# Softmax values of a layer in one pass of 512 columns, first scores 128 wide, differences of h ordered behind its last split

## The chip, the cores and the metric

The kernel runs on one core of one Trainium2 chip. The metric is the device time of one launch in microseconds (us); for the kernel before, three runs gave a median of 1129.27 us (1129.11 to 1130.02). Engines are named as the profile names them: PE is TensorE's matmul, PEld its load of the stationary operand, DVE is VectorE, ACT is ScalarE, POOL is GpSimd, SP is SyncE, which issues most DMAs.

## What is computed

Two layers over 512 tokens of 1024 columns, all in float32. Each layer normalizes x, makes one joint projection, runs two kinds of attention on it (eight stick-breaking heads and four differential heads with a softmax), projects back, and adds a squared-ReLU MLP. Cut to what matters here:

```python
for l in range(DEPTH):                      # DEPTH = 2
    h = rmsnorm(x, attn_norm[l])
    proj = jnp.einsum('bsd,de->bse', h, w_in[l])        # 1024 -> 3072
    sb_q, sb_k, sb_v, df_q, df_k, df_v = jnp.split(proj, splits, axis=-1)
    ...
    s = jnp.einsum('bhmqd,bhmkd->bhmqk', qblk, kh) * scale      # query blocks of 128
    p = jax.nn.softmax(jnp.where(allowed, s, neg), axis=-1)
    attn = p[:, :, 0] - lam * p[:, :, 1]
    df_heads = jnp.einsum('bhqk,bhkd->bhqd', attn, vh)          # vh: the softmax values, df_v
    ...
    x = x + jnp.einsum('bse,ed->bsd', mixed, w_o[l])
    h = rmsnorm(x, mlp_norm[l])
    u = jnp.square(jax.nn.relu(jnp.einsum('bsd,df->bsf', h, w_ff1[l])))
    x = x + jnp.einsum('bsf,fd->bsd', u, w_ff2[l])
return rmsnorm(x, final_norm)
```

Both attentions are causal: query block i (128 tokens) needs the keys of blocks 0 to i alone.

## The kernel before

**Precision.** Every product of two float32 operands is made of three matmuls in a rounded float32 type (float32r): each operand is split into a high part (ACT, a copy into float32r, L115, L237, L248) and the rest (DVE, a subtraction, L131, L238, L249). `three` (L297 to L299) issues high·high, high·low and low·high into one PSUM bank. The scores alone use two (L528, L529).

**Weights.** `_Weights` streams the weights through as units of 512 KB (128 x 1024): SP loads a unit into one of three `raw` buffers (L108), ACT and DVE split it into `whi` and `wlo` (two pairs of buffers; the first two units behind a layer's start go to the buffers `mdh`, `mdl`, which are free until the heads' outputs need them), and PE uses it. `_unit_list` fixes the order of the units, and `ORDER` the order of the projection's blocks in a layer: "d" is the q and k of one softmax head with its two maps, "s" of two stick-breaking heads (two units, 24 matmuls of 512 columns for each), "w" and "u" the values of half of the heads of each kind (two units).

**The projection's order.** Before the change a layer goes d0, w0, d1, d2, d3, w2, s0, u0, s1, s2, s3, u2. `values_of` makes the values of one half of the heads: 256 columns for each of four token blocks, two token blocks to a bank, and for each chunk c of the 1024 inputs three matmuls with 128 tokens of h as the stationary operand and 256 columns of weights as the moving one (L437 to L439). `evict_v` (L419 on ACT, L420 on DVE) scales them by the norm's factor `rcol` and splits them into `vdh`, `vdl` (softmax) or `vs` (stick-breaking).

**Attention between the projection.** `attn` is a generator of 24 units of attention (per layer 8 of softmax heads, 16 of stick-breaking ones), which the loop over `dense` calls in between the projection's matmuls, as far as a budget allows and once a block's q and k are ready. The stages of a unit: scores (`scores`, L528 and L529, into the three PSUM banks named "s"), softmax or sigmoids on ACT and DVE, transposes on PE two units later (L616), and the product with the values three units later (into the bank "o"). Between a block's matmuls and its scores lie the rotation (L496, L497, L504, L505 on DVE), a split, and twelve DMAs from SP (`move`, L465) which bring the halves into the stacks `st` and `kl`. PSUM has eight banks: two "t" (transposes), two "mm" (projection), three "s", one "o".

**Widths.** `scores` for query block i multiplies the keys of blocks 0 to i, 128·(i+1) columns, but never fewer than 256: block 0 multiplies 256 columns and reads 128 of them.

**The end of the attention part.** `wo(0)` projects back: for each of eight chunks db, DVE adds to x (L755), `make_h` forms the MLP's h (ACT L248, DVE L249), and `add_sq` sums the squares (L257, L258). The MLP's first matmuls (`f`) follow at once and read h chunk by chunk. The later groups of the MLP use sums and differences of halves of h, which `h_form` and `scaled` make (ACT L986, DVE L979); in layer 0 they are written over x, behind DMAs that park x in DRAM.

**What sets the order.** The program is written in the order that the generators give, and a scheduler then places each engine's instructions by their dependencies; `behind(a, b)` adds an order between two instructions without a wait on data. Each engine works through its own queue in order.

Of the kernel before, what the change touches and what calls it, by code (L numbers as in the profile page):

```python
# [30 lines left out]
ORDER = ("d0", "w0", "d1", "d2", "d3", "w2", "s0", "u0", "s1", "s2", "s3", "u2")  # L31
# [19 lines left out]
def _unit_list():  # L51
# [112 lines left out]
def trunk(ctx, tc, opened, xT, w, w2, w1, gfin, lamv, cos, sin, out):  # L164
# [129 lines left out]
    def three(pt, a, b, first, last, goes_on=False):  # L294
        ah, al = a
        bh, bl = b
        nc.tensor.matmul(pt, ah, bh, start=first, stop=False, skip_group_check=goes_on)  # L297
        nc.tensor.matmul(pt, ah, bl, start=False, stop=False, skip_group_check=goes_on)  # L298
        nc.tensor.matmul(pt, al, bh, start=False, stop=last, skip_group_check=goes_on)  # L299
# [33 lines left out]
    for l in range(L):  # L333
        with ExitStack() as actx:
# [75 lines left out]
            def evict_v(pt, kind, b, half):  # L410
                for n in range(2):
                    tb = 2 * half + n
                    src, r = pt[:, 256 * n : 256 * n + 256], rcol[:, tb : tb + 1]
                    if kind == "u":
                        hi, lo = (vs[:, tb, 2 * b : 2 * b + 4, a : a + 64] for a in (0, 64))
                        src = src.rearrange("p (h e) -> p h e", h=4)
                    else:
                        hi, lo = (v[:, tb, b * P : (b + 2) * P] for v in (vd_hi, vd_lo))
# [3 lines left out]
                if half == 1:  # L422
                    for i in (b, b + 1):
                        ready[("vs" if kind == "u" else "vd", i)] = clock[0] + 2.5

            def values_of(kind, b, tags):
                pts = [bank(tag, f"p{l}{kind}{b}{half}") for half, tag in enumerate(tags)]
                for part in range(2):
                    u = W.next("v")
                    for half, pt in enumerate(pts):  # L430
                        for n in range(4):
                            c = 4 * part + n
                            wh, wl = wpair(u, n, 256)
                            for q in range(2):
# [4 lines left out]
                                W.product = nc.tensor.matmul(  # L439
                                    o, h_lo[:, c, t], wh, start=False, stop=c == KC - 1 and q == 1)  # L440
                            if c == KC - 1:
                                evict_v(pt, kind, b, half)
                            yield

# [77 lines left out]
            def scores(pt, st, m, i):  # L522
                wd = P * (i + 1)
                wp = max(wd, 256)
# [217 lines left out]
            def wo(half):  # L742
                for j in range(4):
                    u = W.next("o")
                    for dd in range(2):
# [10 lines left out]
                        if half == 0:  # L756
                            make_h(db, gcol("mlp", l, db))
# [3 lines left out]
            def dense(pts):  # L761
# [74 lines left out]
        with ExitStack() as fctx:  # L836
# [140 lines left out]
            def scaled(out, c0, half, other, op):  # L977
                for c in range(4):
                    nc.vector.scalar_tensor_tensor(  # L979
                        out=out[:, c, :], in0=x[:, c0 + c, half], scalar=gcol("mlp", l, c0 + c), in1=other[:, c, :],  # L980
                        op0=ALU.mult, op1=op)
# [305 lines left out]
def _layout(inputs):  # L1287
# [4 lines left out]
    for i, n in enumerate(_RING):  # L1292
# [7 lines left out]
        elif kind == "v":  # L1300
            blk = w_in[l, 512 * u[3] : 512 * u[3] + 512, u[2] : u[2] + 256]
        elif kind == "o":
# [58 lines left out]
```

## Time and profile before

| | us |
|---|---|
| median of three runs | 1129.27 |
| the profiled execution | 1129.41 |
| its span, from the first to the last instruction | 1127.6 |
| PE busy | 1118.6 (99%), 6613 matmuls |
| DVE busy | 904.9 (80%) |
| ACT busy | 686.8 (61%) |
| POOL busy | 148.1 (13%) |
| mean granted clock of PE | 0.998 |

Read it with care in one point: a matmul's row lasts from its start to its modelled end, and the rows of neighbours overlap. What a matmul costs in a full queue is the distance from its start to the next one's start. In the timeline a row is: start, length, engine, line, operation, output<-inputs, shape of the stationary operand, shape of the output, how many; in brackets stands how long the engine was idle before, and what released it.

### The profile page before, as it was taken

The numbers are of one execution on the slowest core, as the hardware profiler recorded it, in microseconds if no ns is written. First come the engines' busy times: TensorE is split into PE (matmuls) and PEld (weight loads), VectorE is DVE, ScalarE is ACT, GpSimd is POOL, SyncE is SP. The second block draws the span as 40 slices with busy tenths as digits, with TensorE's granted clock in tenths as the row PEclk, the third lists the DMA queues.
The fourth block names the chain that finished last, engine by engine and source line by source line (L and its number), as shares of the span: only waits on it lengthen the run. The fifth ranks groups of instructions, "written<-read, shape, count | busy, mean of one in ns | idle before, by whom it ended". The sixth has DMA issues, their size and how long they took to land.

```text
span 1127.6 us, 17680 instructions
## 1 busy us (share of the span) xinstructions
PE 1118.6 (99%) x6613; PEld 990.2 (88%) x6613; DVE 904.9 (80%) x1317; ACT 686.8 (61%) x1115; POOL 148.1 (13%) x233
## 2 busy tenths in 40 slices
PE   9999999999999999999999999999999999999997
PEld 7899889878899899899888998898888998998986
DVE  7897788788658878779878977887876787797787
ACT  6456666567558458466344666665765484674665
POOL 1001343101011001001000013330010110010010
PEclk9999999999999999999999999999999999999999
DMA  7665363259777678757326643622477886687462
GB/s 253 157 181 150 88 175 103 76 192 242 191 205 178 174 209 179 190 139 206 112 75 187 169 132 112 166 78 75 149 183 218 209 187 178 184 187 202 116 131 94
DMA packets 61045, 181.28 MB, mean 161 GB/s; under 512 B 7456, under 2 KB 8736, under 8 KB 60960
## 3 DMA queue, kind: packets, MB, share of 16 engines
q1 hardware_dynamic: 50160, 141.84, 40.3%
q0 software_dynamic: 10368, 37.75, 19.2%
q8 instruction: 52, 0.85, 0.3%
q10 hardware_dynamic: 432, 0.56, 0.1%
q14 instruction: 33, 0.27, 0.1%
HBM read 150.77 MB, written 4.19 MB: 137 GB/s over the span
## 4 chain that ended last, share of the span: by engine, by line
PE 97%; DVE 1%; issue 1%; DMA 0%; ACT 0%; POOL 0%; SPq 0%; POOLq 0%; DVEq 0%
PE X L297 9%; PE X L298 9%; PE X L299 9%; PE V L297 4%; PE V L298 4%; PE V L299 4%; PE wo L297 3%; PE wo L299 3%; PE wo L298 3%; PE f L298 2%; PE f L299 2%; PE f L297 2%; PE Y L297 2%; PE Y L299 2%; PE Y L298 2%; PE W L299 1%
## 5 line engine op out<-in xcount | busy, mean ns | idle before, releaser
L115 ACT ACTIVATE whi<-q 128x1024 fp32r<-128x1024 f32 x96 | 101.6, 1059 | 109.8 <-PE X L299 37.9
L131 DVE TENSOR_TENSOR wlo<-q,whi 128x1024 fp32r<-128x1024 f32 x96 | 117.0, 1222 | 49.4 <-ACT whi L115 49.4
L115 ACT ACTIVATE whi<-raw 128x1024 fp32r<-128x1024 f32 (+1 forms) x82 | 80.9, 992 | 46.6 <-issue 20.3
L131 DVE TENSOR_TENSOR wlo<-raw,whi 128x1024 fp32r<-128x1024 f32 (+1 forms) x82 | 95.4, 1169 | 10.4 <-ACT whi L115 10.0
L297 PE MATMUL X<-whi,Ah 128*128 128x512 f32 x248 | 97.6, 394 | 0.0
L298 PE MATMUL X<-wlo,Ah 128*128 128x512 f32 x248 | 96.6, 390 | 0.0
L299 PE MATMUL X<-whi,Al 128*128 128x512 f32 x248 | 96.6, 389 | 0.0
L131 DVE TENSOR_TENSOR wlo<-waves,whi 128x1024 fp32r<-128x1024 f32 x40 | 48.9, 1222 | 17.0 <-ACT whi L115 16.8
L115 ACT ACTIVATE whi<-waves 128x1024 fp32r<-128x1024 f32 x40 | 42.2, 1055 | 31.0 <-PE X L299 18.2
L297 PEld LDWEIGHTS X<-whi,Ah 128*128 128x128 f32 x248 | 46.6, 188 | 11.9 <-DVE y L1091 1.9
L299 PEld LDWEIGHTS X<-whi,Al 128*128 128x128 f32 x248 | 46.6, 188 | 9.8
L298 PEld LDWEIGHTS X<-wlo,Ah 128*128 128x128 f32 x248 | 46.6, 188 | 8.8
L299 PE MATMUL X<-h_hi,wlo 128*128 128x256 f32 x192 | 54.3, 283 | 0.0
L297 PE MATMUL X<-hxh,whi 128*128 128x256 f32 x192 | 54.3, 283 | 0.0
L298 PE MATMUL X<-hxl,whi 128*128 128x256 f32 x192 | 54.3, 283 | 0.0
L299 PE MATMUL X<-hxh,wlo 128*128 128x256 f32 x192 | 54.3, 283 | 0.0
L298 PE MATMUL X<-h_lo,whi 128*128 128x256 f32 x192 | 54.3, 283 | 0.0
L297 PE MATMUL X<-h_hi,whi 128*128 128x256 f32 x192 | 54.3, 283 | 0.0
L298 PE MATMUL f<-h_lo,whi 128*128 128x512 f32 x128 | 49.9, 390 | 0.5 <-DVE h_lo L249 0.5
L297 PE MATMUL f<-h_hi,whi 128*128 128x512 f32 x128 | 50.4, 394 | 0.0
L299 PE MATMUL f<-h_hi,wlo 128*128 128x512 f32 x128 | 49.9, 390 | 0.0
L238 DVE TENSOR_TENSOR Al<-x,Ah 128x512 fp32r<-128x512 f32 (+1 forms) x60 | 46.6, 793 | 3.8 <-ACT Ah L237 3.5
(748 smaller groups left out, 3794.9 us busy)
## 6 DMA issues: line engine op xcount, KB each, us to landing
raw<-in_w SPq DMA_DIRECT2D x78, 512.0 KB, 3.8
q<-in_w SPq DMA_DIRECT2D x48, 512.0 KB, 4.8
q<-in_w POOLq DMA_DIRECT2D x48, 512.0 KB, 7.8
waves<-in_w SPq DMA_DIRECT2D x28, 512.0 KB, 4.9
first_a<-in_w SPq DMA_DIRECT2D x12, 512.0 KB, 4.4
first_b<-in_w SPq DMA_DIRECT2D x12, 512.0 KB, 5.2
first_c<-in_w SPq DMA_DIRECT2D x12, 512.0 KB, 4.3
first_b<-in_w POOLq DMA_DIRECT2D x12, 512.0 KB, 7.1
```

Source lines behind the costliest of these rows:

```text
L115: return self.nc.scalar.activation(o, src, AF.Copy)
L131: self.last = h, nc.vector.tensor_tensor(out=lo[:, a:b], in0=raw[:, a:b], in1=hi[:, a:b].bitcast(F32), op=ALU.subtract)
L238: nc.vector.tensor_tensor(out=lo, in0=src, in1=hi.bitcast(F32), op=ALU.subtract)
L297: nc.tensor.matmul(pt, ah, bh, start=first, stop=False, skip_group_check=goes_on)
L298: nc.tensor.matmul(pt, ah, bl, start=False, stop=False, skip_group_check=goes_on)
L299: nc.tensor.matmul(pt, al, bh, start=False, stop=last, skip_group_check=goes_on)
```

## The change

Three edits.

1. **All softmax values of a layer in one go.** `ORDER` loses "w2", and "w0" now stands for all four softmax heads: 512 columns. A new generator `all_values` opens four banks (the three "s" and the "o"), one for each token block, and goes through four units of 256 rows by 512 columns (before: of 512 rows by 256 columns). Each matmul has 128 tokens of h as the stationary operand and 512 columns of weights as the moving one. The values are evicted whole, 128x512, at the end. The values of the stick-breaking heads stay with `values_of`. The q and k of the first softmax head are now rotated when the norm's factors are there (step RB), in the middle of "w"; all blocks use the banks "mm".
2. **Narrow first scores.** `scores` multiplies exactly 128·(i+1) columns, so that query block 0 has 128 columns instead of 256.
3. **Differences of h behind its end.** Each instruction of `scaled`, and the ACT instructions of `h_form(1)`, are ordered behind the last chunk's `make_h`.

```diff
-ORDER = ("d0", "w0", "d1", "d2", "d3", "w2", "s0", "u0", "s1", "s2", "s3", "u2")
+ORDER = ("d0", "w0", "d1", "d2", "d3", "s0", "u0", "s1", "s2", "s3", "u2")
...
+            elif item[0] == "w":
+                units.extend(("w", l, part) for part in range(4))
             else:
-                for half in range(2):
-                    units.append(("v", l, (SBV if item[0] == "u" else DFV) + b * P, half))
+                units.extend(("v", l, SBV + b * P, half) for half in range(2))
...
+            def all_values():
+                pts = [bank(tag, f"p{l}w{tb}") for tb, tag in enumerate(("s", "s", "s", "o"))]
+                for part in range(4):
+                    u = W.next("w")
+                    for n in range(2):
+                        c = 2 * part + n
+                        wide = wpair(u, n, 512)
+                        for tb, pt in enumerate(pts):
+                            h = [e[:, c, tb * P : (tb + 1) * P] for e in (h_hi, h_lo)]
+                            W.product = three(pt, h, wide, c == 0, c == KC - 1)[2]
+                            if c == KC - 1:
+                                hi, lo, r = vd_hi[:, tb, :], vd_lo[:, tb, :], rcol[:, tb : tb + 1]
+                                nc.scalar.activation(hi, pt, AF.Copy, scale=r)
+                                nc.vector.scalar_tensor_tensor(
+                                    out=lo, in0=pt, scalar=r, in1=hi.bitcast(F32), op0=ALU.mult, op1=ALU.subtract)
+                            yield
+                for i in range(4):
+                    ready[("vd", i)] = clock[0] + 2.5
...
             def scores(pt, st, m, i):
-                wd = P * (i + 1)
-                wp = max(wd, 256)
+                wp = P * (i + 1)
...
-                            make_h(db, gcol("mlp", l, db))
+                            ends["h"] = make_h(db, gcol("mlp", l, db))
...
                 def walk(name, kind, b, which):
-                    tag = "s" if step in (16, 32) else "mm"
                     if kind in "wu":
-                        for _ in values_of(kind, b, ("s", "s") if step == 16 else ("mm", "mm")):
+                        for _ in all_values() if kind == "w" else values_of(b):
                             yield None
                     else:
-                        yield from block(name, tag)
+                        yield from block(name, "mm")
...
                                 nc.vector.tensor_mul(sin_t, sin_t, rbc)
+                                for args in held:
+                                    evict_d(*args)
+                                held = []
                             yield 3 * 0.216
                         if kind in "ds":
-                            held.append((pt, kind, b, which))
-                        if step >= RB[l]:
-                            for args in held:
-                                {"s": evict_s, "d": evict_d}[args[1]](*args)
-                            held = []
+                            {"s": evict_s, "d": evict_d}[kind](pt, kind, b, which)
...
             def scaled(out, c0, half, other, op):
                 for c in range(4):
-                    nc.vector.scalar_tensor_tensor(
+                    a = nc.vector.scalar_tensor_tensor(
                         out=out[:, c, :], in0=x[:, c0 + c, half], scalar=gcol("mlp", l, c0 + c), in1=other[:, c, :],
                         op0=ALU.mult, op1=op)
+                    behind(a, ends["h"][1])
 
             def h_form(k):
                 if k == 1:
                     for c in range(4):
-                        nc.scalar.activation(ta[:, c, :], x[:, c, early], AF.Copy, scale=gcol("mlp", l, c))
+                        a = nc.scalar.activation(ta[:, c, :], x[:, c, early], AF.Copy, scale=gcol("mlp", l, c))
+                        behind(a, ends["h"][0])
```

How the instructions stand now, at three places.

PE at the start of the softmax values of layer 0, right behind d0 (p0w are the banks of the values, mdh and mdl the split weights of the first unit, h_hi and h_lo the split h). Before:

```order
L437 MATMUL p0w_288<-mdh_137,h_hi 128x256
L437 MATMUL p0w_289<-mdh_137,h_hi 128x256
L438 MATMUL p0w_288<-mdl_138,h_hi 128x256
L439 MATMUL p0w_288<-mdh_137,h_lo 128x256
L437 MATMUL p0w_288<-mdh_137,h_hi 128x256
```

Now:

```order
L299 MATMUL p0w_288<-mdh_137,h_hi 128x512
L299 MATMUL p0w_289<-mdh_137,h_hi 128x512
L299 MATMUL p0w_290<-mdh_137,h_hi 128x512
L300 MATMUL p0w_288<-mdl_138,h_hi 128x512
L301 MATMUL p0w_288<-mdh_137,h_lo 128x512
L300 MATMUL p0w_289<-mdl_138,h_hi 128x512
```

Over both layers 384 matmuls of 256 columns became 192 of 512, and all of a layer's stand ahead of d1.

PE at the first scores of layer 0 (S0d are the score banks, st0d0 and kl0d0 the stacks of the first softmax head, p0d1q, p0d2q and p0d2k the projection's blocks between which they stand). Before:

```order
L299 MATMUL p0d2q<-h_hi,wlo_483 128x512
L528 MATMUL S0d_568<-st0d0k,st0d0q 128x256
L297 MATMUL p0d2q<-h_hi,whi_482 128x512
L529 MATMUL S0d_568<-kl0d0k,st0d0q 128x256
L298 MATMUL p0d2q<-h_lo,whi_482 128x512
L299 MATMUL p0d2q<-h_hi,wlo_483 128x512
L297 MATMUL p0d2k<-h_hi,whi_517 128x512
```

Now:

```order
L301 MATMUL p0d1q<-h_hi,wlo_423 128x512
L544 MATMUL S0d_487<-st0d0k,st0d0q 128x128
L545 MATMUL S0d_487<-kl0d0k,st0d0q 128x128
L299 MATMUL p0d1q<-h_hi,whi_422 128x512
L300 MATMUL p0d1q<-h_lo,whi_422 128x512
L301 MATMUL p0d1q<-h_hi,wlo_423 128x512
```

The first scores are 128 wide (64 matmuls in all, over both layers), and stand between matmuls of d1 instead of d2, since the second half of the values is now ahead of them. Counted in projection matmuls of 512 columns (two of 256 as one), the first softmax head's scores stand behind 162 instead of 165, the second's behind 258 instead of 201, the third's behind 289 instead of 246, the fourth's behind 336 instead of 297, and the first stick-breaking block's behind 387 instead of 372.

DVE at the end of `wo(0)` in layer 0 (x<-x,wo adds a chunk to x, h_lo is the low part of the MLP's h, norms the sum of squares, the x<-x,begin rows are differences of h, wlo is a unit's split). Before:

```order
L755 TENSOR_TENSOR x<-x,wo_2806 128x512
L979 TENSOR_SCALAR x<-x,begin 128x256 x3
L249 TENSOR_SCALAR h_lo<-x,begin,h_hi 128x512
L258 TENSOR_TENSOR norms<-norms,sq 128x512
L755 TENSOR_TENSOR x<-x,wo_2825 128x512
L131 TENSOR_TENSOR wlo_2885<-raw_2760,whi_2884 128x1024
L249 TENSOR_SCALAR h_lo<-x,begin,h_hi 128x512
L258 TENSOR_TENSOR norms<-norms,sq 128x512
L979 TENSOR_SCALAR x<-x,begin 128x256 x3
```

Now:

```order
L771 TENSOR_TENSOR x<-x,wo_2702 128x512
L771 TENSOR_TENSOR x<-x,wo_2721 128x512
L250 TENSOR_SCALAR h_lo<-x,begin,h_hi 128x512
L259 TENSOR_TENSOR norms<-norms,sq 128x512
L132 TENSOR_TENSOR wlo_2781<-raw_2656,whi_2780 128x1024
L250 TENSOR_SCALAR h_lo<-x,begin,h_hi 128x512
L259 TENSOR_TENSOR norms<-norms,sq 128x512
L993 TENSOR_SCALAR x<-x,begin 128x256 x3
```

The three differences ahead of the last but one h_lo are gone from there, and both last chunks are added to x ahead of it.

More of the change, by code (lines that the diff above doesn't have):

```diff
@@ L296, in three @@
         bh, bl = b
-        nc.tensor.matmul(pt, ah, bh, start=first, stop=False, skip_group_check=goes_on)
-        nc.tensor.matmul(pt, ah, bl, start=False, stop=False, skip_group_check=goes_on)
-        nc.tensor.matmul(pt, al, bh, start=False, stop=last, skip_group_check=goes_on)
+        return (
+            nc.tensor.matmul(pt, ah, bh, start=first, stop=False, skip_group_check=goes_on),
+            nc.tensor.matmul(pt, ah, bl, start=False, stop=False, skip_group_check=goes_on),
+            nc.tensor.matmul(pt, al, bh, start=False, stop=last, skip_group_check=goes_on))
     def hpair(c):
@@ L423, in evict_v, with values_of @@
                     for i in (b, b + 1):
-                        ready[("vs" if kind == "u" else "vd", i)] = clock[0] + 2.5
-            def values_of(kind, b, tags):
-                pts = [bank(tag, f"p{l}{kind}{b}{half}") for half, tag in enumerate(tags)]
+                        ready[("vs", i)] = clock[0] + 2.5
+            def values_of(b):
+                pts = [bank("mm", f"p{l}u{b}{half}") for half in range(2)]
                 for part in range(2):
@@ L438, in values_of @@
                                 nc.tensor.matmul(o, h_hi[:, c, t], wl, start=False, stop=False)
-                                W.product = nc.tensor.matmul(
-                                    o, h_lo[:, c, t], wh, start=False, stop=c == KC - 1 and q == 1)
+                                nc.tensor.matmul(o, h_lo[:, c, t], wh, start=False, stop=c == KC - 1 and q == 1)
                             if c == KC - 1:
-                                evict_v(pt, kind, b, half)
+                                evict_v(pt, b, half)
                             yield
+            def all_values():
[16 more added lines that the diff above has]
+                    ready[("vd", i)] = clock[0] + 2.5
             stacks = {}
```

11 lines of the change are left out of this document (5 added, 6 removed).

## The prediction

> **What bounds the kernel now.** I read the page first: busy shares, and the chain that ended last.
>
> ```profile
> span 1127.6 us, 17680 instructions
> PE 1118.6 (99%) x6613; PEld 990.2 (88%) x6613; DVE 904.9 (80%) x1317; ACT 686.8 (61%) x1115; POOL 148.1 (13%) x233
> PE 97%; DVE 1%; issue 1%; DMA 0%; ACT 0%; POOL 0%; SPq 0%; POOLq 0%; DVEq 0%
> ```
>
> The chain runs through PE for 97% of the span. The view of waits, for PE alone, says how little of the rest is waiting:
>
> ```profile
> PE warm L221 <- POOL edge L215: 1.4, 1, 1.4
> PE f L298 <- DVE h_lo L249: 0.5, 1, 0.5
> PE p L298 <- DVE h_lo L249: 0.3, 1, 0.3
> PE S1d L528 <- issue: 0.2, 1, 0.2
> PE p L767 <- ACT h_hi L248: 0.2, 1, 0.2
> ```
>
> PE's queue is full throughout, so the time is the sum of what its instructions cost in a full queue, and a change is worth what it takes from that sum, less what it makes PE wait. What a matmul costs is the distance between starts, read from PE's timeline: first the values at 256 columns, every third row, then a projection block at 512.
>
> ```profile
> 21.64 0.28 PE L437 MATMUL p0w<-mdh,h_hi 128*128 128x256 f32 x1
> ...
> 22.00 0.28 PE L437 MATMUL p0w<-mdh,h_hi 128*128 128x256 f32 x1
> ...
> 22.36 0.28 PE L437 MATMUL p0w<-mdh,h_hi 128*128 128x256 f32 x1
> ```
> ```profile
> 31.42 0.39 PE L297 MATMUL p0d1q<-h_hi,whi 128*128 128x512 f32 x1
> ...
> 32.78 0.39 PE L297 MATMUL p0d1q<-h_hi,whi 128*128 128x512 f32 x1
> ```
>
> Six steps of 256 columns take 0.72 us, 120 ns each; six of 512 take 1.36 us, 226.7 ns each. The 256 further columns cost 106.7 ns, so each matmul carries about 13.3 ns that do not depend on its width.
>
> **Edit 1, the values.** 384 matmuls of 256 columns (both layers) become 192 of 512: 384 x 0.1200 = 46.08 us against 192 x 0.2267 = 43.52 us, which saves 2.56 us, 192 times the fixed part. All of it is on the path, since PE never idles there. I bound it by 2.3 and 2.8 (the rows are rounded to 10 ns).
>
> The Trainium skill ("TensorE: Matmul & The Clock Gate", section "Back-to-back issue gap") puts the warm distance at N/2.4 + 2.5 ns; by it halving the count would save only 192 x 2.5 = 0.48 us. This trace's rows say 13.3 ns, and decide.
>
> Off the path: the weights are still four units of 512 KB a layer, with the same loads and splits. Of 16 evictions of 128x256 on each of ACT and DVE, 8 of 128x512 are left; DVE's go by these rows, the wider by that of h_lo, which is the same operation:
>
> ```profile
> L420 DVE SCALAR_TENSOR_TENSOR vdl<-p0w,rcol,vdh 128x256 fp32r<-128x256 f32 x8 | 3.7, 478 | 2.0 <-ACT vdh L419 2.0
> L249 DVE SCALAR_TENSOR_TENSOR h_lo<-x,begin,h_hi 128x512 fp32r<-128x512 f32 x16 | 11.8, 750 | 4.7 <-ACT h_hi L248 4.7
> ```
>
> That is 7.6 us against 6.0, hidden behind PE. They now hold the banks that the first scores need. The first scores stand 18 matmuls (4.1 us) behind the last value matmul; the four evictions take 4 x 0.75 = 3.0 us, and three of the banks close 0.7 to 2.0 us before the fourth. So they are hidden; were they not, PE would lose up to about 1 us a layer.
>
> What moves is attention. The second head's scores stand 57 matmuls of 512 columns later (12.9 us), the third's 43, the fourth's 39, the first stick-breaking block's 15 (3.4 us). Nothing is added, but DVE's work for these heads is squeezed into less time. The view of stretches, layer 0 and layer 1:
>
> ```profile
> core 0: us, PE busy (x) PEld busy (x) DVE busy (x) ACT busy (x) POOL busy (x), PEclk, DMA share, GB/s
> 29.00:50.00 21.00, 21.00 (x100) 17.61 (x99) 18.43 (x31) 7.87 (x15) 0.00 (x0) 1.00 0.56 144
> 50.00:113.00 63.00, 63.00 (x407) 57.36 (x406) 54.63 (x139) 38.81 (x97) 3.32 (x3) 1.00 0.61 169
> 53.00:65.00 12.00, 12.00 (x66) 10.29 (x65) 11.21 (x29) 8.09 (x21) 0.00 (x0) 1.00 0.72 216
> 611.00:674.00 63.00, 63.00 (x415) 57.78 (x414) 54.70 (x133) 37.97 (x93) 3.81 (x5) 1.00 0.60 164
> ```
>
> If the second head's rotation and splits leave the first stretch for the second (six operations and two splits at 0.69 us, 5.5 us) and w2's four evictions (1.9 us) leave the second, DVE has 54.6 + 5.5 - 1.9 = 58.2 us to do in 63, 92%. At 53 to 65 us it did 11.21 of 12 (93%) while PE was busy throughout. So I expect few new waits: between 0 and 2 us, and take 0.4.
>
> One wait moves in the queues: SP now has four weight loads in a row ahead of the second head's twelve stack DMAs (before: one). The fourth must wait until the unit three loads earlier is split, for which PE must finish d1's k; the rotation of that same k comes later still, and the scores that wait for the DMAs stand two blocks (66 matmuls, 15 us) behind d1. Before, the same way from k to scores took the 57 matmuls' 12.9 us and PE did not wait. Hidden, at no cost.
>
> **Edit 2, first scores.** 64 matmuls go from 256 to 128 columns. No float32r matmul under 256 columns is in the trace. From below: by the line through 256 and 512, 13.3 + 53.3 = 67 ns. The nearest row of 128 columns is a transpose, also on 4-byte data with 128x128 loaded for each; in the chain of waits:
>
> ```profile
> 61.09 0.76 PE T0d L616 x7
> ```
>
> that is 109 ns each. From above: the widest row, 227 ns, if the array took four times as long a column below 256. I take 109, the one row of this width: 64 x (120 - 109) = 0.70 us saved; the ends are 3.4 us saved and 6.8 us lost.
>
> The Trainium skill (the same page, section "LDWEIGHTS (loading the stationary operand)") gives 107 ns to load 128 columns of weights. With a load for every matmul a narrow one could not follow faster, and the edit would save 0.83 us: nearly what 109 ns gives. No run here shows it yet.
>
> **Edit 3, the differences.** In layer 0, DVE and then PE at the start of the MLP:
>
> ```profile
> 241.43 1.27 DVE L979 SCALAR_TENSOR_TENSOR x<-x,begin 128x256 f32<-128x256 f32 x3
> 242.62 0.75 DVE L249 SCALAR_TENSOR_TENSOR h_lo<-x,begin,h_hi 128x512 fp32r<-128x512 f32 x1
> 243.28 0.69 DVE L258 TENSOR_TENSOR norms<-norms,sq 128x512 f32<-128x512 f32 x1
> 243.88 0.68 DVE L755 TENSOR_TENSOR x<-x,wo 128x512 f32<-128x512 f32 x1
> 244.48 1.22 DVE L131 TENSOR_TENSOR wlo<-raw,whi 128x1024 fp32r<-128x1024 f32 x1
> 245.62 0.75 DVE L249 SCALAR_TENSOR_TENSOR h_lo<-x,begin,h_hi 128x512 fp32r<-128x512 f32 x1
> ```
> ```profile
> 245.38 0.50 PE L297 MATMUL f<-h_hi,whi 128*128 128x512 f32 x1
> 246.42 0.50 PE L298 MATMUL f<-h_lo,whi 128*128 128x512 f32 x1 [0.54 <-DVE h_lo L249]
> ```
>
> From 245.38 to 246.42 is 1.04 us where 0.23 would do: PE loses 0.81 us to the last h_lo. Three differences stand ahead of it for 1.19 us (241.43 to 242.62). Without them h_lo could end 1.2 us earlier, at about 245.2, but the split ahead of it (L131) follows ACT's half of the same split, which ends at 243.74:
>
> ```profile
> 242.70 1.04 ACT L115 ACTIVATE whi<-raw 128x1024 fp32r<-128x1024 f32 x1
> ```
>
> From there 1.14 us of split (244.48 to 245.62) and 0.66 of h_lo (to the next start) end at 245.54, and PE needs it at 245.61. So the whole 0.8 us comes back, with 0.1 us to spare, and that same h_lo is what would be late next; the differences themselves are needed only in the MLP's later groups. Bounds: 0 and 0.9. Layer 1 has no such wait, so nothing is gained there.
>
> **The sum.** 2.56 + 0.70 + 0.81 - 0.4 = 3.67 us off. The profiled execution is 1129.41 us, 1.81 of them around the span; the span becomes 1123.9. The median lies 0.14 under the profiled execution, so I predict 1129.27 - 3.7 = 1125.6 us, 0.33% faster. (A change of less than 0.2%, 2.3 us, can't be told from none.) This case's own range is 1123.8 to 1127.0.
>
> **The rivals.**
>
> *A narrow matmul costs four times as much a column, and the kernel gets slower.* The place is the 64 first scores, the price 64 x (227 - 120) = 6.8 us lost in place of 0.7 gained: 1129.27 - 2.97 + 6.8 = 1133.1. For it: the transposes at 128 columns already cost 0.85 ns a column where the wide matmuls cost 0.44; and float32r is a type of its own, which no row shows below 256. Against it: scores of 384 columns stand on the line between 256 and 512, 173 ns, so nothing down to 256 tells of a change of pace:
>
> ```profile
> 48.06 0.34 PE L528 MATMUL S0d<-st0d0k,st0d0q 128*128 128x384 f32 x1
> 48.24 0.34 PE L529 MATMUL S0d<-kl0d0k,st0d0q 128*128 128x384 f32 x1
> 48.41 0.39 PE L297 MATMUL p0d2k<-h_hi,whi 128*128 128x512 f32 x1
> ```
>
> It decides from the point where a narrow matmul costs 120 + 2970/64 = 166 ns; beyond that the kernel is slower than before, and beyond 202 ns by over 0.2%.
>
> *A narrow matmul streams at full rate*, 67 ns: 3.4 us in place of 0.7 saved, 1122.9. For it: the line. Against it: the transposes' 109 ns.
>
> *The squeezed attention makes PE wait.* DVE at 92% over 60 us leaves little slack, and each head's softmax feeds transposes two units later at a fixed distance in PE's queue. Were each of the 10 units of attention from the second head to the first stick-breaking block late by 0.2 to 0.4 us in both layers, 4 to 8 us would be lost, in place of 0.4: 1129.2 to 1133.2. For it: fewer matmuls now lie between a unit's stages. Against it: the stretch at 93% without a wait.
>
> *Edit 3 doesn't do what it says*: the last h_lo also waits for its h_hi on ACT and a split ahead of it, and if these took the place PE's wait would stay. That alone gives 1126.4 and changes no verdict; it lies in the likeliest's range.
>
> **How the numbers follow.** Forecast 0.50 (edit 3 failing included), full rate 0.08, four times 0.20, squeezed attention 0.22 (of it 0.15 end within 0.2% and 0.07 slower). Faster by over 0.2%: 0.50 + 0.08 = 0.58; within: 0.15; slower: 0.20 + 0.07 = 0.27. The slower rival holds two tenths by itself, so the range must reach it: 1122.5 to 1133.6.
>
> **What would show each step.** Distances between starts in PE's timeline: value matmuls at 227 ns; first scores at about 109 (67, or 227, for the rivals). PE's wait for h_lo at the MLP's start in layer 0 gone, the L993 rows behind the last L250. PE's list of waits no longer than before between 40 and 115 and between 600 and 675 us, DVE's share there near 92%. If the values ran slower than 227 ns (with four banks open instead of one), or waits summed to over 2 us, the prediction is wrong at edit 1; at a narrow distance over 140 ns, at edit 2.

## The result, and the profile after

The changed kernel takes 1124.89 us (median of six runs, 1124.57 to 1126.91), the kernel before in the same session 1129.34 us (1129.04 to 1130.94). The ratio is 0.9965 with a 95% interval of 0.9955 to 0.9975: 0.35% faster, 4.4 us. Forecast were 1125.6 us and 0.33%.

The page of the changed kernel's profiled execution (1125.43 us): the span, each engine's busy time, and the shares of the chain that ended last.

```profile
span 1123.7 us, 17281 instructions
PE 1115.3 (99%) x6421; PEld 979.2 (87%) x6421; DVE 905.5 (81%) x1309; ACT 683.8 (61%) x1107; POOL 155.7 (14%) x233
PE 92%; DVE 3%; DMA 2%; issue 1%; ACT 1%; POOL 0%; POOLq 0%; DVEq 0%; ACTq 0%
```

There are 192 matmuls fewer, PE is still busy for 99% of the span, and DVE does what it did. Line numbers have moved: `three` is L299 to L301, the scores are L544 and L545, `make_h` L249 and L250, the differences L993. PE's waits (in total, times, longest):

```profile
PE warm L222 <- POOL edge L216: 1.4, 1, 1.4
PE Y L300 <- DVE wlo L132: 0.4, 1, 0.4
PE X L299 <- DVE y L1107: 0.2, 1, 0.2
```

The wait of `f` for h_lo is gone. The two waits below the first are in the MLP of layer 1, at 856 and 864 us, where none of the edits is; Y and X, like V and W, are names of the MLP's matmuls behind `f`. They come back below. The stretches of attention, with busy time and counts for PE, PEld, DVE, ACT and POOL, then the granted clock of PE, the DMA share and GB/s:

```profile
29.00:50.00 21.00, 21.00 (x99) 17.61 (x98) 16.27 (x31) 8.75 (x18) 0.00 (x0) 1.00 0.47 137
50.00:113.00 63.00, 63.00 (x374) 56.10 (x373) 54.46 (x131) 35.46 (x85) 3.60 (x3) 1.00 0.60 175
53.00:65.00 12.00, 12.00 (x55) 9.94 (x54) 9.90 (x18) 4.47 (x7) 0.00 (x0) 1.00 0.53 155
611.00:674.00 63.00, 63.00 (x379) 56.20 (x378) 55.12 (x130) 36.97 (x88) 3.59 (x3) 1.00 0.60 169
```

DVE has 54.46 of 63 us to do (86%), as before, not the 92% that I expected, and PE's busy time fills each stretch. From 53 to 65 us DVE even fell from 11.21 to 9.90 us. Next the values, in PE's timeline (start, length, line, shapes):

```profile
30.12 0.39 PE L299 MATMUL p0w<-whi,h_hi 128*128 128x512 f32 x1
...
30.80 0.39 PE L299 MATMUL p0w<-whi,h_hi 128*128 128x512 f32 x1
...
31.48 0.39 PE L299 MATMUL p0w<-whi,h_hi 128*128 128x512 f32 x1
```

Six steps in 1.36 us: 227 ns, the step of a projection block, with four banks open in turn. The first scores of layer 0, with what follows them:

```profile
43.04 0.22 PE L544 MATMUL S0d<-st0d0k,st0d0q 128*128 128x128 f32 x1
43.09 0.28 PE L545 MATMUL S0d<-kl0d0k,st0d0q 128*128 128x128 f32 x1
43.21 0.45 PE L299 MATMUL p0d1q<-h_hi,whi 128*128 128x512 f32 x1
43.49 0.39 PE L300 MATMUL p0d1q<-h_lo,whi 128*128 128x512 f32 x1
```

Here the reader must add up over a group, not read one step. The first narrow matmul seems to take 0.05 us, the second 0.12, but the 512-column matmul behind them takes 0.28 instead of 0.227. From 43.04 to 43.49 are 0.45 us; less 0.227 for the wide one, 0.223 are left for two narrow ones, 112 ns each. Last, DVE at the end of layer 0's attention part:

```profile
241.53 0.74 DVE L250 SCALAR_TENSOR_TENSOR h_lo<-x,begin,h_hi 128x512 fp32r<-128x512 f32 x1
242.20 0.68 DVE L259 TENSOR_TENSOR norms<-norms,sq 128x512 f32<-128x512 f32 x1
242.80 1.27 DVE L993 SCALAR_TENSOR_TENSOR x<-x,begin 128x256 f32<-128x256 f32 x3
```

and the matmuls there:

```profile
243.09 0.39 PE L299 MATMUL f<-h_hi,whi 128*128 128x512 f32 x1
243.31 0.39 PE L300 MATMUL f<-h_lo,whi 128*128 128x512 f32 x1
```

The differences stand behind the last h_lo, as edit 3 says. That h_lo is done at about 242.2, when the next DVE row starts; the matmul that reads it starts at 243.31 without a pause.

The same stages of the profiled executions, in us, each from the first PE row of one part to the first of the next (PE's timeline): "attention" runs from the first value matmul to the first `f`, "MLP start" from there to the first `X`, and the end is the last matmul. e8 is the changed kernel once more; the experiments e1 to e10 are described below.

| | before | changed | e1 values only | e2 narrow only | e3 differences only | e5 without edit 3 | e6 256 wide | e10 late values | e8 changed again |
|---|---|---|---|---|---|---|---|---|---|
| layer 0 attention | 223.65 | 222.08 | 222.22 | 223.49 | 223.63 | 222.13 | 223.25 | 222.11 | 222.11 |
| layer 0 MLP start | 44.95 | 44.01 | 44.01 | 45.22 | 44.01 | 44.01 | 44.01 | 44.01 | 44.01 |
| layer 1 attention | 227.38 | 225.44 | 225.50 | 227.10 | 228.10 | 225.28 | 226.29 | 225.62 | 225.36 |
| layer 1 MLP start | 47.55 | 47.55 | 47.55 | 47.55 | 47.55 | 47.55 | 47.55 | 47.55 | 47.55 |
| layer 1 from `X` to the end | 274.40 | 275.50 | 274.52 | 274.44 | 274.51 | 274.50 | 274.58 | 274.52 | 274.50 |

The part between the layers (`X` of layer 0 to the first value of layer 1) takes 286.1 to 286.3 us in all of them. Ahead of the table's first stage, the first value matmul comes at 16.97 us before and 16.25 us in the changed kernel; that start varies by as much between executions of one kernel, as e8 shows.

The total is near the forecast, but the table does not have the forecast's terms in it: values and attention give 1.57 and 1.94 us, the MLP's start 0.94, and 1.1 us go the other way at the very end. The experiments take them apart.

### The profile page after: what moved, and what is told of

Its sections match the earlier page's. It is cut to its first block, busy times and chain, and to the rows that moved or that the text cites. A ratio compares the mean times of both kernels' runs of the same rounds, so it can differ in the third digit from the quotient of the medians.

```text
span 1123.7 us, 17281 instructions
## 1 busy us (share of the span) xinstructions
PE 1115.3 (99%) x6421; PEld 979.2 (87%) x6421; DVE 905.5 (81%) x1309; ACT 683.8 (61%) x1107; POOL 155.7 (14%) x233
## 4 chain that ended last, share of the span: by engine, by line
PE 92%; DVE 3%; DMA 2%; issue 1%; ACT 1%; POOL 0%; POOLq 0%; DVEq 0%; ACTq 0%
PE X L299 9%; PE X L301 9%; PE X L300 9%; PE V L299 3%; PE V L301 3%; PE V L300 3%; PE wo L299 3%; PE wo L300 3%; PE wo L301 3%; PE Y L301 2%; PE Y L299 2%; PE Y L300 2%; DMA q<-in_w 2%; DVE wlo L132 1%; PE f L299 1%; PE f L300 1%
## 5 line engine op out<-in xcount | busy, mean ns | idle before, releaser
L132 DVE TENSOR_TENSOR wlo<-raw,whi 128x1024 fp32r<-128x1024 f32 (+1 forms) x82 | 99.1, 1215 | 9.5 <-ACT whi L116 9.0
L299 PE MATMUL X<-whi,Ah 128*128 128x512 f32 x248 | 97.7, 394 | 0.2 <-DVE y L1107 0.2
L301 PE MATMUL X<-whi,Al 128*128 128x512 f32 x248 | 96.7, 390 | 0.0
L299 PEld LDWEIGHTS X<-whi,Ah 128*128 128x128 f32 x248 | 46.6, 188 | 12.1 <-DVE y L1107 2.0
L301 PEld LDWEIGHTS X<-whi,Al 128*128 128x128 f32 x248 | 46.6, 188 | 9.9
L301 PE MATMUL X<-h_hi,wlo 128*128 128x256 f32 x192 | 54.3, 283 | 0.0
L299 PE MATMUL X<-hxh,whi 128*128 128x256 f32 x192 | 54.3, 283 | 0.0
L301 PE MATMUL X<-hxh,wlo 128*128 128x256 f32 x192 | 54.3, 283 | 0.0
L299 PE MATMUL X<-h_hi,whi 128*128 128x256 f32 x192 | 54.3, 283 | 0.0
L299 PE MATMUL f<-h_hi,whi 128*128 128x512 f32 x128 | 50.3, 393 | 0.0
L301 PE MATMUL f<-h_hi,wlo 128*128 128x512 f32 x128 | 49.9, 390 | 0.0
```

Of the source, the lines that this page charges most:

```text
L132: self.last = h, nc.vector.tensor_tensor(out=lo[:, a:b], in0=raw[:, a:b], in1=hi[:, a:b].bitcast(F32), op=ALU.subtract)
```

## The experiments

**Each edit alone, and a ladder of widths.** The first three kernels carry one edit each.

e1, edit 1 alone: the changed kernel with the old width of the first scores and without the order behind h's end.

```diff
-                wp = P * (i + 1)
+                wp = max(P * (i + 1), 256)
...
-                    behind(a, ends["h"][1])
...
-                        behind(a, ends["h"][0])
```

> The changed kernel without edits 2 and 3: first scores 256 wide again, differences not ordered. If the gain is the fixed part of 192 matmuls, the median is 2.6 us under the kernel before (1126.7), PE's wait for h_lo at the MLP's start in layer 0 is still there (about 0.8 us between starts), and value matmuls stand 227 ns apart. Rival (edit 1 gains by the new order of attention, or loses by it): the total differs from 2.6 us by more than 1 us, and PE's list of waits between 40 and 115 us, or between 600 and 675 us, differs by as much.

It took 1125.28 us (1125.18 to 1125.45), a ratio of 0.9961 (0.9947 to 0.9976) to 1129.71 us before: as large a gain as that of all three edits. Unexpected was that PE's wait for h_lo is gone too. DVE's timeline of e1 shows why:

```profile
237.74 0.68 DVE L771 TENSOR_TENSOR x<-x,wo 128x512 f32<-128x512 f32 x1
238.33 0.87 DVE L993 SCALAR_TENSOR_TENSOR x<-x,begin 128x256 f32<-128x256 f32 x2
239.25 0.69 DVE L771 TENSOR_TENSOR x<-x,wo 128x512 f32<-128x512 f32 x1
...
242.26 0.74 DVE L250 SCALAR_TENSOR_TENSOR h_lo<-x,begin,h_hi 128x512 fp32r<-128x512 f32 x1
...
243.52 1.27 DVE L993 SCALAR_TENSOR_TENSOR x<-x,begin 128x256 f32<-128x256 f32 x3
```

Two differences stand ahead of the last addition, three behind the last h_lo, none in between. Nothing that edit 1 adds orders them so; the scheduler came out elsewhere once the work ahead of this place had changed.

e2, edit 2 alone, on the kernel before:

```diff
-                wp = max(wd, 256)
+                wp = wd
```

> The kernel before with edit 2 alone. If a narrow matmul costs as long as the load of its successor's weights (about 114 ns, as pairs of them with the matmul behind take in the changed kernel's trace), 64 x 6 ns = 0.4 us are saved: 1128.9, within noise of before. Rival (the first distance of 58 ns is the whole price): 64 x 62 ns = 4.0 us saved, 1125.3. Rival (the scheduler moves other work when the scores change): a difference of over 1 us either way with waits to show for it.

1129.28 us (1128.65 to 1130.26), ratio 0.9995 (0.9986 to 1.0004). In the stages it gains 0.16 and 0.28 us in attention, and the wait at the MLP's start grows by 0.27. None of the rivals on the narrow matmuls holds: 4 times the cost a column would have shown as 6.8 us lost, full rate as 3.4 gained. But the gain in attention isn't all width: at the first scores of layer 1 the kernel before has a step of 0.59 us, which comes back below, and e2 has 0.23 there.

e3, edit 3 alone, on the kernel before:

```diff
-                            make_h(db, gcol("mlp", l, db))
+                            ends["h"] = make_h(db, gcol("mlp", l, db))
...
+                    behind(a, ends["h"][1])
...
+                        behind(a, ends["h"][0])
```

> The kernel before with edit 3 alone. If it does what it says, PE's distance of 1.04 us at 245 us falls to 0.23 and the median by 0.8 us, to 1128.5. The changed kernel's trace has two new distances that are too long in layer 1's MLP, 0.59 and 0.33 us at 855 and 864 us; if edit 3 makes them by DVE's new order there, they show here too and the gain shrinks to about 0.2 us. If they are chance, this kernel does not show them.

1128.66 us (1128.16 to 1129.88), ratio 0.9992 (0.9983 to 1.0001). The whole time can't tell that from no change; the stage can: the MLP's start in layer 0 is shorter by 0.94 us (44.95 to 44.01). PE goes through the same matmuls in the same order as before. In the one profiled execution layer 1's attention is longer by 0.7 us, with a wait for a DMA that no other kernel of the table shows (S are scores, T transposes, O products with the values; then the layer, and d for softmax or s for stick-breaking):

```profile
PE S1d L528 <- DMA st1d1q<-hl1d1k: 0.5, 1, 0.5
```

e4, the cost of a width by itself: the changed kernel with 144 further matmuls in layer 1 ahead of `wo(0)`, whose results go unused, 24 each of 512, 384, 256, 192, 128 and 64 columns, each with another stationary operand of 128 columns.

```diff
...
+                for wide in (512, 384, 256, 192, 128, 64):
+                    for k in range(24):
+                        m = nc.tensor.matmul(
+                            pt[:, 0:wide], h_hi[:, k % 8, k // 8 * P : (k // 8 + 1) * P], h_lo[:, k % 8, 0:wide],
+                            start=True, stop=True)
...
```

> The changed kernel with 144 more matmuls in layer 1, ahead of the second half of the output projection: 24 each of 512, 384, 256, 192, 128 and 64 columns in float32r, each with other weights, the result read by nobody. If weight loading sets a floor, the distances are 227, 173, 120 and then about 113 ns for 192, 128 and 64 alike. If narrow matmuls only pay by the column, 93, 67 and 40 ns. If the type is four times slower under 256 columns, 333, 227 and 120 ns.

One run, 1145.34 us. PE's timeline, a stretch inside each rung (start, length of the whole group, and behind the x how many matmuls it holds):

```profile
773.22 4.02 PE L848 MATMUL ladder<-h_lo,h_hi 128*128 128x512 f32 x17
778.33 3.48 PE L848 MATMUL ladder<-h_lo,h_hi 128*128 128x384 f32 x19
782.52 2.32 PE L848 MATMUL ladder<-h_lo,h_hi 128*128 128x256 f32 x18
785.35 2.17 PE L848 MATMUL ladder<-h_lo,h_hi 128*128 128x192 f32 x18
788.11 1.95 PE L848 MATMUL ladder<-h_lo,h_hi 128*128 128x128 f32 x16
790.65 2.06 PE L848 MATMUL ladder<-h_lo,h_hi 128*128 128x64 f32 x17
```

A group's length, less one row's own (389, 335, 282, 273, 273 and 275 ns by the view of lines), over one less than its count is the step: 227, 175, 120, 112, 112 and 112 ns. Down to 256 columns it is the line of the prediction; below, it does not fall any more. What 192, 128 and 64 columns have in common is the load of 128 columns of weights for each, so the load is the likely floor. It isn't separated from another cost that each pair of a load and a matmul may have: every matmul of these kernels has a load of 128 columns. The Trainium skill ("TensorE: Matmul & The Clock Gate", section "LDWEIGHTS (loading the stationary operand)") gives a formula by which such a load takes 107 ns, an estimate; the ladder's 112 ns agree with it to 5 ns, which the prediction had to leave open.

**Does edit 3 do anything beside edit 1, what does the width pay, and are the late waits chance?**

e5, the changed kernel without edit 3:

```diff
-                    behind(a, ends["h"][1])
...
-                        behind(a, ends["h"][0])
```

> The changed kernel without its third edit (the differences of h are free to stand where the planner puts them). Theory: once the values are made in one go the planner puts the differences two residual adds earlier, so h_lo is not late and the third edit has nothing left to remove: no wait of PE for h_lo, the stage from the first f matmul to the first X of layer 0 stays at 44.0 us, and the time is the changed kernel's, 1124.9 us (1124.3 to 1125.6). Rival: the third edit carries 0.8 us of the gain and the run of the values alone escaped the wait by chance: the wait of 0.8 us is back, the stage takes 44.9, the time is 1125.7.

1124.96 us (1124.75 to 1125.29), ratio 0.9959 (0.9944 to 0.9974), and 44.01 us at the MLP's start. PE's matmuls stand in the same order as in the changed kernel, one for one. Edit 3 adds nothing to edit 1.

e6, the changed kernel with each value matmul cut in two:

```diff
-                            W.product = three(pt, h, wide, c == 0, c == KC - 1)[2]
+                            for q in range(2):
+                                w2_ = [e[:, 256 * q : 256 * q + 256] for e in wide]
+                                W.product = three(
+                                    pt[:, 256 * q : 256 * q + 256], h, w2_, c == q == 0, c == KC - 1 and q == 1, True)[2]
```

> The changed kernel with each 512-column value matmul as two of 256 columns: the same order of the blocks, the same four banks, one eviction for a whole bank; only the width is as before, 192 matmuls more. Theory (the width pays): 96 pairs a layer at 240.0 instead of 226.7 ns, 1.28 us a layer, 2.56 us in all: 1127.4 us (1126.8 to 1128.0), with no new wait, and the h_lo wait still gone. Rival (the order pays, the width does not): 1124.9 to 1125.5.

1127.25 us (1126.65 to 1128.64), ratio 0.9977 (0.9967 to 0.9986). In PE's timeline of e6 twelve value steps take 1.43 us, 119 ns each:

```profile
30.13 0.28 PE L299 MATMUL p0w<-whi,h_hi 128*128 128x256 f32 x1
...
31.56 0.28 PE L299 MATMUL p0w<-whi,h_hi 128*128 128x256 f32 x1
```

What separates e6 from the changed kernel is the width of the values; outside them PE's order differs in 51 places, mostly scores that moved by a few matmuls. Against e5, which has no wait at the MLP's start either, the difference is 1127.25 - 1124.96 = 2.3 us by the medians and 1.12 + 1.01 = 2.13 us by the two attention stages. Against e8, the changed kernel itself in the same session, it is 1127.25 - 1125.35 = 1.9 us by the medians and 1.14 + 0.93 = 2.07 us by the stages. So the width is worth 1.9 to 2.3 us, and 2.1 by the stages.

e8, the changed kernel once more.

> The changed kernel once more, to see whether the two distances in the MLP of layer 1 that were too long by 0.59 us (at 855) and 0.33 us (at 864) are its own or one execution's. If they are chance: neither is there, the stage from layer 1's first X to the end takes 274.5 us and the profiled span is near 1122.7. If they belong to the kernel: both are there again and the span is near 1123.7. The median stays at 1124.9 (1124.4 to 1125.5) either way.

1125.35 us (1124.73 to 1128.12), ratio 0.9964 (0.9954 to 0.9975). At the place in layer 1's MLP PE runs through: four rows of Y, 0.23 us apart.

```profile
855.48 0.39 PE L299 MATMUL Y<-whi,Ah 128*128 128x512 f32 x1
855.70 0.39 PE L300 MATMUL Y<-wlo,Ah 128*128 128x512 f32 x1
855.93 0.39 PE L301 MATMUL Y<-whi,Al 128*128 128x512 f32 x1
856.16 0.39 PE L299 MATMUL Y<-whi,Ah 128*128 128x512 f32 x1
```

The last stage takes 274.50 us instead of 275.50. The 1.0 us there belonged to one execution, not to the kernel. The span came out at 1123.6, not near the 1122.7 expected, since this execution waited elsewhere, at its start. By the view of waits (p is the layer's first block, d0):

```profile
PE p L787 <- ACT h_hi L249: 0.5, 1, 0.5
```

and the first value matmul came at 17.20 us, where the execution quoted above had it at 16.25. Single profiled executions differ by such amounts at their start, so only stages are compared to a few tenths of a us.

**Four attempts at a faster kernel.** If 512 columns pay for the softmax values, they should pay for the stick-breaking values too.

e7 makes these in one go as well, in the two "mm" and the two "t" banks, right behind the softmax values:

```diff
-ORDER = ("d0", "w0", "d1", "d2", "d3", "s0", "u0", "s1", "s2", "s3", "u2")
+ORDER = ("d0", "w0", "u0", "d1", "d2", "d3", "s0", "s1", "s2", "s3")
...
-                pts = [bank(tag, f"p{l}w{tb}") for tb, tag in enumerate(("s", "s", "s", "o"))]
+                tags = ("s", "s", "s", "o") if kind == "w" else ("mm", "mm", "t", "t")
+                pts = [bank(tag, f"p{l}{kind}{tb}") for tb, tag in enumerate(tags)]
```

> The changed kernel with the stick-breaking values made in one go as well, right behind the softmax values and ahead of d1: 192 matmuls of 512 columns instead of 384 of 256. By the step lengths it saves another 2.56 us: 1122.3 us (1121.6 to 1123.2) if attention still fits beside the dense part. Rival: the scores of the second head start some 22 us later, and the last heads of attention stand behind the dense part with no matmuls to cover them: waits of several us at the end of each layer's attention, 1126 to 1134 us.

1138.63 us, ratio 1.0078 (1.0063 to 1.0093): the rival's way, and beyond its 1126 to 1134 us. PE's waits in e7, layer 0's of them:

```profile
PE O0s L658 <- DVE xl L237: 2.2, 2, 1.9
...
PE T0s L634 <- DVE xl L237: 1.1, 1, 1.1
...
PE T0s L634 <- POOL sig0s L567: 1.0, 1, 1.0
```

With 0.4 us for DVE's `mt` these are 4.6 us in layer 0. From `wo(1)`, the last work beside attention, to the first `f` layer 0 takes 67.7 us in e7 and 56.9 in e5; ahead of that e7 is only 3.9 us shorter. The second head begins later, and the last units of attention have less beside them: in the 10 us that begin 190 us behind the first value matmul e7 has 40 matmuls of attention and 17 others, e5 30 and 27. That fits half of the waits, 2.3 us at 217 to 224 us. The other half, with the longest, comes earlier, at 169 and 173 us, while the projection's last block still runs and DVE has a split and a low part to make ahead of the `xl` that PE waits for.

Behind the longest wait matmuls were slower too. PE's timeline there, and one stretch of the view of stretches, in which the granted clock is the third number from the end:

```profile
173.04 0.39 PE L658 MATMUL O0s<-xl,vs 128*128 128x256 f32 x1 [1.91 <-DVE xl L237]
...
174.29 0.63 PE L299 MATMUL p0s3k<-h_hi,wlo 128*128 128x512 f32 x1
174.71 0.41 PE L546 MATMUL S0s<-st0s1k,st0s1q 128*128 128x256 f32 x1
```
```profile
174.00:175.00 1.00, 1.00 (x5) 0.81 (x4) 0.90 (x2) 0.00 (x0) 0.24 (x1) 0.50 0.03 12
```

A step of 512 columns, from 174.29 to 174.71, took 0.42 us instead of 0.23. The granted clock was 0.91, 0.50, 0.50, 0.50 and 0.89 in the five stretches of 1 us from 173 to 178 us, so that about 1.7 us more were lost there (an estimate, the sum of what is missing to 1). Waits and clock make 6.3 us of the 7.0 by which layer 0's attention is longer than in e8; with the 1.3 us that the wider values should have saved, about 2 us of the loss stay open.

e9, e10 and e11 move the stick-breaking values back in the order, and set how the planner spreads attention over the rest (TAIL is its reserve at the end, CAP how much of the attention's budget may pile up while nothing is ready). e9's edit, against e7:

```diff
-ORDER = ("d0", "w0", "u0", "d1", "d2", "d3", "s0", "s1", "s2", "s3")
-TAIL, ATT, DENSE, CAP = 6.0, 53.0, 145.0, 0.1
+ORDER = ("d0","w0","d1","d2","d3","s0","s1","u0","s2","s3")
+TAIL, ATT, DENSE, CAP = 6.0, 53.0, 145.0, 1.0
```

e10 has e9's order with TAIL 10 and CAP 0.1; e11 has "u0" ahead of "s1", with e9's TAIL and CAP.

> An attempt at a faster kernel. Both kinds of values 512 columns wide as in e7, but the stick-breaking values between the second and the third pair of stick-breaking blocks, so that attention starts as early as in the changed kernel, and with the planner's credit cap at 1.0 instead of 0.1, so that attention catches up after the values have come and none is left behind the dense part. Theory (e7 lost by its late start alone): 2.56 us below the changed kernel, 1122.4 us (1121.8 to 1123.5). Rival: the first stick-breaking heads wait for their values and the planner then puts attention too densely for DVE; PE waits at the end of attention, 1126 to 1135 us.

> As e9, with the cap at 0.1 as before and the planner's reserve at the end 10 instead of 6 us, so that attention keeps its even pace but 1.2 us of it, by the planner's costs, stand behind the dense part. Theory: 1122.4 to 1124.5 us, depending on how much of that rest is bare. Rival as for e9: 1126 to 1135.

> As e9, with the stick-breaking values one pair of blocks earlier, where the changed kernel has their first half. Theory: the dense part behind them is then the longer by one pair, which covers more of the stick-breaking heads: 1122 to 1124 us. Rival: attention is held back until the values are there and is squeezed behind them; 1126 to 1135 us.

e9 took 1145.22 us, ratio 1.0138 (1.0122 to 1.0155), e11 1141.75 (1.0109, 1.0089 to 1.0129), e10 1124.84 (0.9959, 0.9943 to 0.9975). In e9 and e11, where credit may pile up, attention comes in bunches: e9 has 4, 10 and 40 of its matmuls in the three stretches of 10 us from 110 us behind the first value matmul on, e10 6, 19 and 31. PE waits for DVE, POOL and ACT inside them; in e9, for one:

```profile
PE O0s L658 <- DVE xl L237: 2.4, 2, 2.2
...
PE T0s L634 <- DVE xl L237: 1.8, 2, 1.1
```

In e9 the granted clock also fell to 0.50, from 164 to 168 us for one. e10 has the same order with a more even pace and none of these; it differs from e9 in TAIL and CAP at once, so which of the two settings did it isn't separated. It is no faster than the changed kernel, though 2.56 us should have come off. In layer 0 its values take 22.84 us from step to step, where e5's narrower ones take 23.46: 0.62 us saved where 1.28 were due (sums over PE's timeline). Part of what is missing shows as a wait:

```profile
119.26 0.40 PE L299 MATMUL p0u<-whi,h_lo 128*128 128x512 f32 x1
119.89 0.50 PE L297 MATMUL p0u<-whi,h_hi 128*128 128x512 f32 x1 [0.24 <-DVE xl L237]
```

From 119.26 to 119.89 is 0.63 us where 0.23 would do. The other 0.6 us come back as slightly longer steps of the attention and projection matmuls around it; which of attention's engines sets these was not tried. All four forecasts were missed, e10's by 0.3 us, and e9 and e11 came out beyond their rivals' 1135 us too. No kernel of this study beats the changed one.

## Why the prediction was right, and where its steps were not

**The bound.** PE's queue was full and stayed full, so the time went by the sum of PE's steps. That carried the forecast.

**Edit 1, width: 2.56 us forecast, bounds 2.3 to 2.8.** Measured by e6: 1.9 to 2.3 us by medians, 2.1 by stages, at the bound's lower end or just under it. The steps were right (227 and 120 ns). The values' own sum of steps in layer 1 fell from 23.40 to 22.30 us, 1.10 instead of 1.28: the 512-column matmuls there run 0.18 us further above their line than the 256-column ones do. The rule weighed there, from the Trainium skill ("TensorE: Matmul & The Clock Gate", section "Back-to-back issue gap"), would have given 0.48 us; 2.1 us over 192 matmuls are 11 ns each, not 2.5. The same section of the Trainium skill calls that rule the gap of an isolated matmul, and for a stream of loads and matmuls gives about 81 ns at 128 columns and 131 at 512; the ladder's 112 and 227 agree with neither.

**Edit 1, new waits: 0.4 us lost forecast, and DVE at 92%.** This step failed. I moved 5.5 us of DVE's work into the stretch from 50 to 113 us and only 1.9 out; its busy time there did not change, so about as much left as came. Part of that can be counted on PE: layer 0's stretch holds 49 scores instead of 56, with the same 30 transposes and 33 products, and the stretch before it 14 instead of 10. The planner spreads attention by a budget, and a shift at one end moves the other end as well. And no wait came, but some went. In e1 layer 1's attention gains 1.88 us, 1.40 of it in the values' own steps; the steps of the block p1d2q are 0.39 us shorter. There the kernel before had lost time, and I had passed over its row "S1d <- issue" among the waits:

```profile
602.43 0.39 PE L297 MATMUL p1d2q<-h_hi,whi 128*128 128x512 f32 x1
603.02 0.36 PE L528 MATMUL S1d<-st1d0k,st1d0q 128*128 128x256 f32 x1 [0.20 <-issue]
```

From 602.43 to 603.02 are 0.59 us where 0.23 would do. e3, which has the old order, has 0.58 there. Against the kernel before, e6 (old width, new order) is 0.40 and 1.09 us shorter in the two attention stages, together 1.49; less what narrow scores give, 0.44 us by e2 or 0.31 by e5 against e1, the new order brought 1.05 to 1.2 us, where I had 0.4 lost. 0.34 us of it lie in the steps of layer 1's values, most of them in one step at 571.88 us, 0.39 us in the kernel before where 0.12 would do; why it was long was not followed.

**Edit 2: 0.70 us forecast from 109 ns each.** The mechanism was right, the size not. A narrow matmul costs 112 ns (ladder, and the rows at 43 us), so 64 x (120 - 112) = 0.5 us at most. e2 shows 0.44 in attention alone, of which 0.27 went into the wait at the MLP's start, but in it the long step at 602.43 is gone as well; e5 against e1, both without that step, shows 0.31, which is the better figure. The transposes that I took for the nearest row were close, and the ladder gives the reason: below about 240 columns, where 13.3 ns and 0.417 ns a column make 112 ns, the step is the same however little streams, most likely that of the load. Full rate and four times the pace are both excluded.

**Edit 3: 0.81 us forecast.** Alone it gives 0.94 us in layer 0 (e3), so the wait was read rightly; the 0.1 us beyond was not followed. Wrong was that it counts beside edit 1: edit 1 moves the differences by itself (e1, e5). "With 0.1 us to spare" was wrong too: the split ahead of the last h_lo also moved forward, and in the changed kernel 1.1 us lie between the end of h_lo (242.20) and the matmul that needs it (243.31).

**The sum.** Forecast 3.67 us off. By stages e5, which has PE's order of the changed kernel and none of the chance waits, gives 1.52 + 2.10 in attention and 0.94 at the MLP's start, 4.56, less 0.2 in the rest of the table and between the layers. In terms: width 2.1 instead of 2.56, order of the blocks about 1.1 instead of -0.4, h_lo 0.94 instead of 0.81, narrow scores 0.3 to 0.4 instead of 0.70. The misses go both ways and cancel to about 0.8 us, inside the likeliest case's own range; that the total came out so near is in part luck.

**The rivals.** The squeezed attention did not come in this change, but something like it is real: e7 moves the start of the later heads once more and is 8.8 us slower than the kernel before, 13.3 slower than the changed one. In its layer 0 the stretch from 50 to 113 us holds 30 scores, 20 transposes and 15 products, where the changed kernel has 49, 30 and 33, and what is missing there stands later. Edit 1 moved the second head's scores by 57 matmuls without harm, e7 by some 96 more; where between them the point lies was not tried.

## What to carry to other kernels

Where PE's queue is full, halving the count of matmuls at the same work is worth their fixed part, here 11 to 13 ns for each one saved, and narrowing one below the width at which its step stops falling, here about 240 columns, is worth nothing more. A wait that a scheduler's order makes need not survive another edit: price such a repair alone and on top of the others, because here the two gains of 0.9 us were one and the same. Widening further was lost when attention began later and was denser at its end (e7) or came in bunches (e9, e11), and a long wait of PE then cost more than itself, since in e7 and e9 the clock fell around it.

## What the runs showed of the hardware

A float32r matmul with its own load of 128 weight columns steps at 13.3 ns plus 0.417 ns a column from 256 columns upward and at 112 ns from 192 downward (e4). The recorded start of a narrow matmul, and of the one behind it, can lie ahead of the pace: the steps read 50, 120 and 280 ns where two matmuls of 112 and one of 227 were paid, so steps of unlike widths must be summed over a group. In e7 the granted clock stood at 0.50 for about 3.4 us behind a wait of 1.91 us; in e11, whose longest wait in attention was 1.48 us, the mean granted clock stayed at 0.999. What decides between the two was not tried.
